# Differential attention: value products of a unit's first three groups follow their transposes by four groups, not three

## The chip, the cores and the metric

The kernel runs on one core of one Trainium2 chip. The metric is the device time of one execution in microseconds (us). Five engines work beside each other, each through its own queue in order: TensorE (PE in the profile, its weight loads PEld), VectorE (DVE), ScalarE (ACT), GpSimd (POOL) and SyncE (SP), which issues DMA transfers. They wait for one another through semaphores.

## The reference

The program is one step of a two-layer backbone over 2048 latent and 256 prompt tokens. Each layer has three head groups side by side; the change touches the first, differential attention with 4 heads:

```python
s = jnp.einsum('bqhcd,bkhcd->bhcqk', qblk, k).astype(jnp.float32) * scale
p = jax.nn.softmax(s, axis=-1)
w = p[:, :, 0] - lam * p[:, :, 1]
return jnp.einsum('bhqk,bkhd->bqhd', w.astype(v.dtype), v)
```

Every head has two score matrices (c = 0 and 1, of 64 channels each). Their softmaxes are combined into one weight matrix w, and w times the values (128 channels) is the output, which is then normalised and scaled. A latent query sees 2048 latent and 256 context keys, 2304 in all; a prompt query sees the 256 prompt keys.

## The kernel before

**Units.** Attention of a layer is cut into 36 units (list `units`): 4 heads, and of each head 8 blocks of 256 latent queries and, in the fifth place, one block of 256 prompt queries. Units are numbered from 0; units 4, 13, 22 and 31 are the prompt units.

**Scores.** `scores(i)` makes a latent unit's scores in 12 chunks: 2 query tiles j, 2 score matrices c, 3 pieces of 768 keys. A chunk is 4 matmuls into a psA buffer (line 882; psA has two buffers), which VectorE evicts with a running minimum (line 885). After three chunks comes the minimum over them, nb (line 889), and one exponential over 2304 columns on ScalarE, which also gives the sum z (line 890). After both matrices of a query tile, `combine` forms cf from the sums (reciprocal, line 935; product, line 936) and adds the second matrix to the first in three column sections: VectorE (line 945), ScalarE with GpSimd (lines 949 and 953), GpSimd alone (lines 952 and 953).

**Turns and products.** The combined weights lie with queries on the partitions, so they are transposed in groups of 256 keys. `turn(i, g)` makes the 4 transposes of a group (line 968) into one of three psT banks in rotation, and copies them out: for groups 0 to 5 a rounded part wh (ScalarE, line 977) and the rest wl (VectorE, line 978), each in a ring of three buffers; for groups 6 to 8 one f32 copy wf (ScalarE, line 973), two buffers. `product(i, g)` multiplies them with the values: 6 matmuls for a split group (lines 999 to 1001), 4 matmul passes for an f32 group (line 992). All nine products of a unit accumulate in one psT bank, `tb[0]`. The last one is followed by ScalarE's copy of this bank to oT (line 1007), so the next unit's first product has to wait for that copy. A unit's groups are taken in the order `ORDER`; the text calls their turns the 1st to the 9th. Groups 6, 7 and 8 are the 3rd, 6th and 9th.

**Output.** The last product also puts `output` on the list `later`, due two ticks on: two transposes of oT (line 1013) into the next of the three rotating banks, the copy ob, sums of squares, and GpSimd's scale; `finish`, due three ticks after it, multiplies and stores.

**What sets the order.** The loop behind `for _ in stepper` emits one chunk (one step of `scores`) at a time and adds `RATE` = 0.75 to a credit; with a credit of 1 it calls `advance`, which emits one turn and then, if more than `BACK` = 3 turns are waiting for their product, the product of the oldest. So 12 chunks go with 9 turns, and a product follows its own turn by three turns. After every `advance` the tick is raised by one, and what in `later` is due is emitted. The matmuls and transposes are pinned (`pin`): TensorE runs them in the order in which they are emitted. The instructions of VectorE and ScalarE in attention aren't pinned; the compiler's planner orders them. Scores run ahead of the turns of the same unit by one unit and some steps (`LAG`).

Of the kernel before, what the change touches and what calls it, by code (L numbers as in the profile page):

```python
# [13 lines left out]
F32R = mybir.dt.float32r  # L14
# [5 lines left out]
P = 128  # L20
# [19 lines left out]
DEFER = 3  # L40
ORDER = (0, 1, 6, 2, 3, 7, 4, 5, 8)
BACK = 3
SIDE = (1.02, 0.45)
SIDE_FROM = 2

# [32 lines left out]
def hybrid_backbone(ctx: ExitStack, tc: tile.TileContext, ins, outs):  # L78
# [8 lines left out]
    def nm(s):  # L87
        uid[0] += 1
        return f"{s}_{uid[0]}"
# [249 lines left out]
    for l in range(DEPTH):  # L339
# [266 lines left out]
        def sw_tiles(t):  # L606
            if t >= NT:
                return [NT + 2, NT + 3], 0
            b0, b1 = max(t - 1, 0), min(t + 1, NT - 1)
            return list(range(b0, b1 + 1)) + [NT, NT + 1], (b1 + 1 - b0) * P  # L610
# [104 lines left out]
        items = deque((t, i) for t in range(NALL) for i in range(len(sw_tiles(t)[0])))  # L715
        turned, later, ready = deque(), deque(), {}
# [87 lines left out]
        def v_slot(h, i):  # L804

            if i == 2:
                return (xslot, yslot)[h % 2][:, 6912:7680].rearrange("p (t d) -> p t d", d=P)
            o = (2 * h + i) % 3 * 1536
            return vslot[:, o:o + 1536].rearrange("p (a t d) -> p a t d", a=2, d=P)
# [5 lines left out]
        def p_slot():  # L815
            v = vslot[:, 4608:5632]
            return (v[:, 0:512].rearrange("p (c n) -> p c n", c=2),
                    v[:, 512:1024].rearrange("p (a t n) -> p a t n", a=2, t=2))
# [11 lines left out]
        def load_v(h, i):  # L830
            v1 = v_slot(h, i) if i == 2 else v_slot(h, i).bitcast(F32)
            if i == 2:
                hs = slice(h * P, (h + 1) * P)
                nc.sync.dma_start(out=v1[:, 0:4], in_=vfscr[l][:, :, hs].rearrange("t p d -> p t d"))
                nc.sync.dma_start(out=v1[:, 4:6],
                                  in_=c_dv[0, l].rearrange("(t p) h d -> p t h d", p=P)[:, :, h, :])
                return
            for a in range(2):
                nc.sync.dma_start(out=v1[:, a], in_=vscr[l][a, 6 * i:6 * i + 6, :, h * P:(h + 1) * P]
                                  .rearrange("t p d -> p t d"))  # L840
# [116 lines left out]
        def turn_bank():  # L957
            n_t[0] += 1
            return tb[1 + n_t[0] % 3]

        def turn(i, g):
            h, p = units[i]
            st = state[i]
            pt = turn_bank()
            for kk in range(2):
                for j in range(2):
                    o = (2 * kk + j) * P
                    pin(nc.tensor.transpose(out=pt[:, o:o + P],  # L968
                                            in_=st["s"][j][:, (2 * g + kk) * P:(2 * g + kk + 1) * P],
                                            identity=ident))  # L970
            if g >= 6:
                wh, wl = at.tile([P, 512], F32, tag="wf", name=nm("wf"), bufs=2), None
                nc.scalar.activation(wh, pt, AF.Copy)
            else:
                wh = at.tile([P, 512], F32R, tag="wh", name=nm("wh"), bufs=3)
                wl = at.tile([P, 512], F32R, tag="wl", name=nm("wl"), bufs=3)
                nc.scalar.activation(wh, pt, AF.Copy)  # L977
                nc.vector.tensor_tensor(wl, pt, wh.bitcast(F32), op=ALU.subtract)  # L978
            st[g] = wh, wl
            if g == groups(i)[-1]:  # L980
                free.extend(st["e"])

        def product(i, g):
            h, p = units[i]
            po = tb[0]
            wh, wl = state[i].pop(g)
            for kk in range(2):
                k = 2 * g + kk
                cs = slice(kk * 256, (kk + 1) * 256)
                last = g == groups(i)[-1] and kk == 1  # L990
                if g >= 6:
                    pin(nc.tensor.matmul(po[:, 0:256], v_slot(h, 2)[:, k % 6, :], wh[:, cs],  # L992
                                         start=False, stop=last))
                    continue
                if p < 8:
                    vh, vl = (v_slot(h, k // 6)[:, a, k % 6, :] for a in range(2))
                else:
                    vh, vl = (p_slot()[1][:, a, k, :] for a in range(2))
                pin(nc.tensor.matmul(po[:, 0:256], vh, wh[:, cs], start=(k == 0), stop=False))  # L999
                pin(nc.tensor.matmul(po[:, 0:256], vh, wl[:, cs], start=False, stop=False))  # L1000
                pin(nc.tensor.matmul(po[:, 0:256], vl, wh[:, cs], start=False, stop=last))
                if p == 7 and h < 3 and k == 5:
                    load_v(h + 1, 1)
            if last:
                st = state.pop(i)
                oT = at.tile([P, 256], F32, tag="oT", name=nm("oT"), bufs=2)
                nc.scalar.activation(oT, po[:, 0:256], AF.Copy)  # L1007
                later.append((tick + 2, lambda: output(h, p, st["ez"], oT)))

        def output(h, p, ez, oT):  # L1010
            pt = turn_bank()
            for j in range(2):
                pin(nc.tensor.transpose(out=pt[:, j * P:(j + 1) * P],
                                        in_=oT[:, j * P:(j + 1) * P], identity=ident))
            ss = at.tile([P, 16], F32, tag="ss", name=nm("ss"), bufs=3)[:, 0:2]
            ob = at.tile([P, 256], F32, tag="ob", name=nm("ob"), bufs=2)
            nc.scalar.activation(ob, pt[:, 0:256], AF.Copy)
            for j in range(2):
                js = slice(j * P, (j + 1) * P)
                nc.scalar.activation(oT[:, js], ob[:, js], AF.Square, accum_out=ss[:, j:j + 1])  # L1020
            nc.gpsimd.tensor_scalar(ss, ss, 1.0 / P, None, op0=ALU.mult)
            nc.gpsimd.tensor_tensor(ez, ez, ss, op=ALU.add)
            nc.gpsimd.tensor_tensor(ez, ez, mhalf.to_broadcast([P, 2]), op=ALU.pow)

            def finish():
                ov = ob.rearrange("p (j n) -> p j n", j=2)
                nc.gpsimd.tensor_tensor(ov, ov, ez.unsqueeze(2).to_broadcast([P, 2, P]), op=ALU.mult)
                rows = slice(2 * p * P, (2 * p + 2) * P)
                nc.sync.dma_start(out=oscr[l][rows, h * P:(h + 1) * P].rearrange("(j p) n -> p j n", p=P),
                                  in_=ov)  # L1030

            later.append((tick + DEFER, finish))

        def groups(i):
            return ORDER if units[i][1] < 8 else (0,)
# [45 lines left out]
        def p3_proj(i, a):  # L1081
# [4 lines left out]
            for k in range(KC):  # L1086
                if i >= SIDE_FROM:
                    due += SIDE[half] * (1 if k else 2)
                while due >= 1.0:
# [178 lines left out]
        at = Pool(tc, f"at{l}", side=near)  # L1268
# [6 lines left out]
        items = deque((i, g) for i in range(len(units)) for g in groups(i))  # L1275
        turned, later = deque(), deque()
# [3 lines left out]
        def advance():  # L1280

            if not items and not turned:
                return False
            if items:
                i, g = items[0]
                if at_ready.get(i, step + 1) > step:
                    return False
                turn(*items.popleft())
                turned.append((i, g))
            if len(turned) > BACK or not items:  # L1290
                product(*turned.popleft())
            return True

        for _ in stepper:
            credit = min(credit + RATE, 2.0)
            while credit >= 1.0 and advance():
                tick += 1
                credit -= 1.0
                while later and later[0][0] <= tick:
                    later.popleft()[1]()  # L1300
# [6 lines left out]
        while advance() or later:  # L1307
            if tick % 2 == 0:
                next(soon, None)
            tick += 1  # L1310
            while later and later[0][0] <= tick:
                later.popleft()[1]()
# [144 lines left out]
```

## Time and profile before

| what | value |
|---|---|
| median of 3 runs | 3640.16 us (3638.21 to 3643.04) |
| the profiled execution, its own time | 3639.05 us |
| span of the profiled execution, first to last instruction | 3637.2 us |
| mean granted TensorE clock | 0.991 |
| TensorE busy | 3507.7 us (96%) |
| VectorE busy | 2266.0 us (62%) |
| ScalarE busy | 1928.8 us (53%) |
| GpSimd busy | 1692.3 us (47%) |

The span is one execution recorded instruction by instruction; the 1.85 us between it and the execution's own time lie around it. Busy times are unions over the instructions of an engine. Matmuls are pipelined, with ends that are modelled: two rows of TensorE can overlap, so the start of a row and the idle time that it names in square brackets, with the engine and line that ended it, say more than its length. A wait is put down to the releaser that came last; very short pauses are not listed as waits.

### The profile page before, as it was taken

The numbers are of one execution on the slowest core, as the hardware profiler recorded it, in microseconds if no ns is written. First come the engines' busy times: TensorE is split into PE (matmuls) and PEld (weight loads), VectorE is DVE, ScalarE is ACT, GpSimd is POOL, SyncE is SP. The second block draws the span as 40 slices with busy tenths as digits, with TensorE's granted clock in tenths as the row PEclk, the third lists the DMA queues.
The fourth block names the chain that finished last, engine by engine and source line by source line (L and its number), as shares of the span: only waits on it lengthen the run. The fifth ranks groups of instructions, "written<-read, shape, count | busy, mean of one in ns | idle before, by whom it ended". The sixth has DMA issues, their size and how long they took to land.

```text
span 3637.2 us, 56156 instructions
## 1 busy us (share of the span) xinstructions
PE 3507.7 (96%) x20512; PEld 3043.4 (84%) x20512; DVE 2266.0 (62%) x4780; ACT 1928.8 (53%) x3192; POOL 1692.3 (47%) x1212
## 2 busy tenths in 40 slices
PE   8999999999999999999999999999999999999999
PEld 4788787888888898888878888889888889988887
DVE  3545665763588888885544232276437888888644
ACT  4432124653588888883223222266437888888511
POOL 3333233235477777762223232232436777777421
PEclk9999999999999999999999999999999999999999
DMA  7656557436412121226646454553533122111453
GB/s 255 195 167 197 173 171 216 128 108 210 124 44 81 46 84 57 69 62 228 223 154 179 139 167 125 163 153 117 179 128 106 61 63 83 48 57 55 143 182 116
DMA packets 397156, 477.83 MB, mean 131 GB/s; under 512 B 38353, under 2 KB 309969, under 8 KB 394321
## 3 DMA queue, kind: packets, MB, share of 16 engines
q1 hardware_dynamic: 385360, 462.71, 40.4%
q10 hardware_dynamic: 11520, 11.54, 0.9%
q8 instruction: 162, 2.65, 0.3%
q14 instruction: 114, 0.93, 0.1%
HBM read 314.75 MB, written 159.38 MB: 130 GB/s over the span
## 4 chain that ended last, share of the span: by engine, by line
PE 74%; DVE 10%; ACT 3%; POOL 3%; issue 3%; DMA 1%; SPq 1%; POOLq 0%; ACTq 0%; DVEq 0%
PE psA L882 10%; PE psT L293 7%; PE psT L295 7%; PE psT L294 7%; PE psT L968 5%; PE psA L293 3%; PE psA L295 3%; PE psA L294 3%; PE psT L301 3%; PE psT L303 3%; PE psT L302 3%; PE psT L992 3%; DVE W L885 2%; PE psT L692 2%; PE psT L999 2%
## 5 line engine op out<-in xcount | busy, mean ns | idle before, releaser
L349 POOL TENSOR_TENSOR hl<-h,hh 128x1024 fp32r<-128x1024 f32 x144 | 354.1, 2459 | 518.5 <-ACT hh L348 409.5
L885 DVE TENSOR_SCALAR_CACHE_REDUCE W<-psA 128x768 f32<-128x768 f32 x474 | 445.8, 951 | 87.6 <-PE psA L882 80.9
L882 PE MATMUL psA<-W,W 128*128 128x512 f32 (+1 forms) x1920 | 425.8, 352 | 17.8 <-DVE W L885 13.2
L890 ACT ACTIVATE W<-W,nb 128x2304 f32<-128x2304 f32 x158 | 351.0, 2221 | 78.2 <-DVE nb L889 77.3
L882 PEld LDWEIGHTS psA<-W,W 128*128 128x128 f32 x1920 | 301.1, 189 | 64.8 <-DVE W L885 24.2
L293 PE MATMUL psT<-W,hh 128*128 128x512 f32 (+1 forms) x864 | 312.3, 362 | 14.3 <-ACT hh L348 9.0
L885 DVE TENSOR_SCALAR_CACHE_REDUCE spool<-psA 128x768 f32<-128x768 f32 x294 | 276.7, 952 | 78.1 <-PE psA L882 55.7
L295 PE MATMUL psT<-W,hl 128*128 128x512 f32 (+1 forms) x864 | 308.8, 358 | 3.7 <-POOL hl L349 3.6
L294 PE MATMUL psT<-W,hh 128*128 128x512 f32 (+1 forms) x864 | 307.9, 356 | 0.1
L968 PE MATMUL psT<-ident,W 128*128 128x128 f32 x1616 | 291.2, 273 | 8.5 <-POOL W L953 6.7
L978 DVE TENSOR_TENSOR wl<-psT,wh 128x512 fp32r<-128x512 f32 x392 | 265.1, 683 | 20.8 <-ACT wh L977 20.0
L348 ACT ACTIVATE hh<-h 128x1024 fp32r<-128x1024 f32 x144 | 151.9, 1055 | 234.6 <-PE psT L294 137.3
L999 PE MATMUL psT<-wh,W 128*128 128x256 f32 x784 | 253.6, 323 | 13.1 <-ACT oT L1007 13.1
L882 PE MATMUL psA<-W 128*128 128x512 f32 (+1 forms) x1152 | 255.4, 351 | 9.5 <-DVE spool L885 5.4
L977 ACT ACTIVATE wh<-psT 128x512 fp32r<-128x512 f32 x392 | 225.5, 588 | 54.8 <-PE psT L968 53.8
L890 ACT ACTIVATE spool<-spool,nb 128x2304 f32<-128x2304 f32 x98 | 217.7, 2221 | 62.8 <-DVE nb L889 62.5
L952 POOL TENSOR_SCALAR W<-W,cf 128x768 f32<-128x768 f32 x70 | 162.6, 2322 | 188.5 <-DVE cf L936 73.9
L293 PE MATMUL psT<-W,mh 128*128 128x512 f32 x576 | 229.6, 399 | 4.8 <-ACT mh L1346 4.8
L293 PE MATMUL psA<-W,hh 128*128 128x512 f32 x576 | 229.7, 399 | 0.0
L968 PEld LDWEIGHTS psT<-ident,W 128*128 128x128 f32 x1616 | 202.7, 140 | 29.4 <-POOL W L953 7.8
L295 PE MATMUL psA<-W,hl 128*128 128x512 f32 x576 | 226.7, 394 | 0.0
L295 PE MATMUL psT<-W,ml 128*128 128x512 f32 x576 | 226.4, 393 | 0.0
(258 smaller groups left out, 9592.8 us busy)
## 6 DMA issues: line engine op xcount, KB each, us to landing
h<-hscr SPq DMA_DIRECT2D x126, 512.0 KB, 4.0
W<-qscr SPq DMA_DIRECT2D x288, 128.0 KB, 2.7
ws<-in_w_in SPq DMA_DIRECT2D x88, 256.0 KB, 3.7
kscr<-kst SPq DMA_DIRECT2D x160, 128.0 KB, 3.2
qscr<-qst SPq DMA_DIRECT2D x72, 256.0 KB, 2.8
szscr<-th SPq DMA_DIRECT2D x72, 256.0 KB, 2.1
qb<-qbscr SPq DMA_DIRECT2D x144, 128.0 KB, 2.9
W<-kscr SPq DMA_DIRECT2D x16, 1152.0 KB, 5.8
```

The source lines that it names most:

```text
L293: nc.tensor.matmul(out, ah[:, ks], w[:, 0, k, :n], start=(k == 0), stop=False)
L294: nc.tensor.matmul(out, ah[:, ks], w[:, 1, k, :n], start=False, stop=False)
L295: nc.tensor.matmul(out, al[:, ks], w[:, 0, k, :n], start=False, stop=(k == KC - 1))
L349: nc.gpsimd.tensor_tensor(hl, h32, hh.bitcast(F32), op=ALU.subtract)
L882: pin(nc.tensor.matmul(pa[:, o:o + wd], q[:, c, a, j * P:(j + 1) * P], ks[:, ch * 768 + o:ch * 768 + o + wd], start=(a == 0), stop=(a == 1)))
L885: nc.vector.tensor_scalar(sc_t[:, ch * 768:(ch + 1) * 768], pa[:, 0:768], -0.125, None, op0=ALU.mult, op1=ALU.min, accum_out=mn[:, ch:ch + 1])
L890: nc.scalar.activation(sc_t, sc_t, AF.Exp, bias=nb[:, j, c:c + 1], scale=-1.0, accum_out=z[:, j, c:c + 1])
L952: eng.tensor_scalar(s[1][:, sl], s[1][:, sl], cf, None, op0=ALU.mult)
L968: pin(nc.tensor.transpose(out=pt[:, o:o + P], in_=st["s"][j][:, (2 * g + kk) * P:(2 * g + kk + 1) * P], identity=ident))
L977: nc.scalar.activation(wh, pt, AF.Copy)
L978: nc.vector.tensor_tensor(wl, pt, wh.bitcast(F32), op=ALU.subtract)
L999: pin(nc.tensor.matmul(po[:, 0:256], vh, wh[:, cs], start=(k == 0), stop=False))
```

## The change

A new constant `AHEAD` = 3 and a helper `back` make the distance between a turn and its product depend on the group's place in the unit: for the first three groups of a unit a product is emitted only when more than four turns are waiting, for the others when more than three are. The rings of wh and wl get a fourth buffer. In one unit this gives: no product with the 4th turn, products of the 1st and 2nd group with the 5th and 6th turn, products of the 3rd and the 4th group together with the 7th turn, and from there on the old distance.

```diff
 BACK = 3
+AHEAD = 3
...
-                wh = at.tile([P, 512], F32R, tag="wh", name=nm("wh"), bufs=3)
-                wl = at.tile([P, 512], F32R, tag="wl", name=nm("wl"), bufs=3)
+                wh = at.tile([P, 512], F32R, tag="wh", name=nm("wh"), bufs=4)
+                wl = at.tile([P, 512], F32R, tag="wl", name=nm("wl"), bufs=4)
...
-            if len(turned) > BACK or not items:
+            if not items:
+                product(*turned.popleft())
+            while turned and len(turned) > back():
                 product(*turned.popleft())
             return True
+
+        def back():
+
+            i, g = turned[0]
+            return BACK + (groups(i).index(g) < AHEAD)
```

## Rows read from the trace of the kernel before

**Rows 1.** Stretches, layer 0 attention: us; busy PE, PEld, DVE, ACT, POOL (instructions); clock; DMA; GB/s

```profile
974.40:1616.10 641.70, 621.58 (x4211) 565.23 (x4208) 553.60 (x1293) 545.27 (x830) 476.70 (x392) 1.00 0.21 63
```

**Rows 2.** Waits of TensorE, whole run: waiter, releaser, us in total, times, longest

```profile
PE psA L882 <- DVE W L885: 17.2, 32, 1.0
PE psT L999 <- ACT oT L1007: 13.1, 20, 1.2
PE psA L882 <- DVE spool L885: 9.7, 16, 1.9
```

**Rows 3.** Stretch table, one unit each of patterns 1, 2, 3 and 4

```profile
994.20:1015.70 21.50, 20.23 (x136) 17.91 (x134) 17.24 (x41) 17.14 (x25) 13.62 (x12) 1.00 0.11 31
1122.30:1143.20 20.90, 20.05 (x136) 18.12 (x135) 17.82 (x41) 17.48 (x26) 14.96 (x13) 1.00 0.31 102
1288.70:1308.30 19.60, 19.60 (x137) 18.14 (x136) 17.13 (x41) 17.16 (x26) 15.00 (x12) 1.00 0.27 90
1450.80:1471.10 20.30, 19.77 (x136) 18.02 (x135) 17.32 (x43) 16.89 (x25) 14.93 (x13) 1.00 0.24 67
```

**Rows 4.** TensorE in order of time, pattern 2: start, us, what, idle before

```profile
1128.04 0.60 PE L968 MATMUL psT<-ident,spool 128*128 128x128 f32 x4
1129.15 0.39 PE L999 MATMUL psT<-wh,W 128*128 128x256 f32 x1 [0.52 <-ACT oT L1007]
...
1129.97 0.38 PE L1013 MATMUL psT<-ident,oT 128*128 128x128 f32 x2
1130.11 1.66 PE L882 MATMUL psA<-W 128*128 128x512 f32 x8
1131.60 0.60 PE L968 MATMUL psT<-ident,spool 128*128 128x128 f32 x4
1131.96 0.36 PE L999 MATMUL psT<-wh,W 128*128 128x256 f32 x1
```

**Rows 5.** ScalarE in order of time, the same unit

```profile
1126.03 2.22 ACT L890 ACTIVATE W<-W,nb 128x2304 f32<-128x2304 f32 x1 [0.63 <-DVE nb L889]
...
1128.73 0.37 ACT L1007 ACTIVATE oT<-psT 128x256 f32<-128x256 f32 x1
```

**Rows 6.** Who waited for the copy oT (us, times); the output's weight load (ns)

```profile
  PEld psT L999: 17.8, 20
...
L1013 PEld LDWEIGHTS psT<-ident,oT x144: 137/139/144, 1001.2 to 3411.8; 128*128 128x128 f32 x144
```

**Rows 7.** TensorE in order of time, the same unit, later

```profile
1132.76 0.88 PE L882 MATMUL psA<-W 128*128 128x512 f32 x4
1133.47 0.60 PE L968 MATMUL psT<-ident,spool 128*128 128x128 f32 x4
1133.91 1.03 PE L992 MATMUL psT<-wf,W 128*128 128x256 f32 x4
1134.59 1.05 PE L882 MATMUL psA<-W 128*128 128x512 f32 x4
1135.47 0.60 PE L968 MATMUL psT<-ident,spool 128*128 128x128 f32 x4
```

**Rows 8.** VectorE in order of time, the same unit

```profile
1131.16 0.95 DVE L885 TENSOR_SCALAR_CACHE_REDUCE W<-psA 128x768 f32<-128x768 f32 x1
...
1135.68 0.96 DVE L885 TENSOR_SCALAR_CACHE_REDUCE W<-psA 128x768 f32<-128x768 f32 x1 [1.04 <-PE psA L882]
...
1139.39 0.16 DVE L935 RECIPROCAL cf<-z 128x1 f32<-128x1 f32 x1
...
1141.40 0.94 DVE L885 TENSOR_SCALAR_CACHE_REDUCE spool<-psA 128x768 f32<-128x768 f32 x1
```

**Rows 9.** TensorE in order of time, a unit of pattern 4

```profile
1460.48 1.57 PE L882 MATMUL psA<-W 128*128 128x512 f32 x8
```

**Rows 10.** VectorE in order of time, the same unit of pattern 4

```profile
1459.73 0.95 DVE L885 TENSOR_SCALAR_CACHE_REDUCE W<-psA 128x768 f32<-128x768 f32 x1
...
1461.39 0.96 DVE L885 TENSOR_SCALAR_CACHE_REDUCE W<-psA 128x768 f32<-128x768 f32 x1 [0.71 <-PE psA L882]
```

## Prediction

> **What bounds the kernel now.** I read the stretch table first. The attention stretch of layer 0 lasts 641.70 us and layer 1 has its like, so attention is some 1283 us of the run, and the change acts only there. TensorE is busy for 621.58 us of it at a granted clock of 1.00, VectorE for 553.60 and ScalarE for 545.27 [rows 1]. TensorE is the bound, with 20 us idle per layer; VectorE has some 14% to spare, but not at every place.
>
> The table of waits says what the idle is [rows 2]. Score chunks waited 48 times for VectorE's eviction, 17.2 and 9.7 us, because psA has two buffers. Products waited 20 times for the copy oT, 13.1 us. Going through the matmuls in order of time I put each wait to the turn (1st to 9th of its unit) ahead of it. Of the chunk waits 31, with 17.9 us, stand after a 9th turn (3.0 us of it at the end of layer 0), 10 with 4.7 us after a 6th, and none after a 4th or 5th. Of the oT waits 18 stand after a 4th turn, ahead of a unit's first product, and two after a 3rd.
>
> The stream repeats, in five patterns that differ in the turns that two chunks follow. Of each layer's 32 latent units, 4 are of pattern 1 (units 0 to 3), 8 of pattern 2 (5 to 12), 8 of pattern 3 (14 to 21), 8 of pattern 4 (23 to 30) and 4 of pattern 5. One unit of each of the first four lasts 21.50, 20.90, 19.60 and 20.30 us, with 1.27, 0.85, 0.00 and 0.53 us of TensorE idle [rows 3]. Pattern 3 runs at TensorE's own pace; the others stall somewhere.
>
> **The wait the change aims at.** In a unit of pattern 2 the transposes of the 4th turn start at 1128.04; the unit's first product follows only at 1129.15, after 0.52 us of idle, then the output's two transposes at 1129.97, then two chunks [rows 4]. ScalarE shows why oT is late: an exponential started at 1126.03 and took 2.22 us, so the copy started at 1128.73 [rows 5].
>
> **Part 1: the first product leaves this place.** It goes behind the next turn. But `output` is due two ticks after the last product, counted in calls of `advance`, and the tick count doesn't change. So behind the 4th turn stands now the pair of transposes that read oT themselves, and TensorE's matmuls are pinned in this order. Nothing in the change makes ScalarE's copy earlier. The output's transposes then wait for the same copy until the same moment: the wait changes its owner, and I put **0 us** for it (bounds: 0, and -13.1 if it went wholly).
>
> At this place the Trainium skill's page "TensorE: Matmul & The Clock Gate" (section "Step-by-step: what each phase is for") says that weight loads are pulled ahead of matmuls in flight. By it a product's load of V would be done under the wait, while an output's load is oT itself, so that each of 20 moved waits would cost 139 ns more, an estimate of +2.8 us, or 3643 in place of 3641. The trace has it otherwise: in the same 20 waits the product's own weight load sat idle too, 17.8 us in all [rows 6], so by the row it is 0, and I take the row.
>
> **Part 2: the new order of blocks.** Starts give the cost of a block by what follows. Turn to product is 0.36 us, product to output 0.82, product to chunk 0.80, output to chunk 0.14 [rows 4, 7]; a turn ahead of an f32 product takes 0.44, the f32 product 0.68, and the chunk behind it 0.88 where one behind a split product takes 0.71 [rows 7]. Old order, 4th to 7th turn, without the chunks' own 0.71: 0.36+0.82+0.14+0.07 (what the pair after an output takes over 2 x 0.71), 0.36+0.80, 0.44+0.68+0.17, 0.36+0.80 = 5.00. New order: 0.44+0.14+0.07, 0.36+0.80, 0.36+0.80, 0.44+0.68+0.80 = 4.89, plus x for a split product right behind an f32 product, which no row shows. x lies between 0 and 0.17, what a chunk pays there. I take 0.08, as a product pays part of such a start behind a turn already: -0.03 a unit, **-2 us** for 64 units (bounds -7 and +4).
>
> **Part 3: chunks come earlier.** This is the part that costs. From the 4th to the 7th turn TensorE has one product less behind it, so the chunks between reach TensorE about 0.8 us sooner, while VectorE frees psA when it did. Pattern 2: after the wait the pair starts at 1129.29 instead of 1130.11, the chunk of 1132.76 at 1131.94. It needs the eviction that started at 1131.16 and took 0.95 [rows 8], and waits for 0.17 us; nothing is marked as idle ahead of this eviction, VectorE was at work, so an earlier chunk doesn't bring it forward. 16 units x 0.17 = 2.7. Pattern 4: the pair of 1460.48 [rows 9] starts at 1459.77, and its second chunk at 1460.48 needs the eviction of 1459.73, which ended at 1460.68 [rows 10]: 0.20 us, x 16 = 3.2. Pattern 1: the chunk after the 6th turn already waits; TensorE comes some 0.7 earlier and VectorE gains about half of it, as the eviction ahead is behind a ScalarE result: 0.35 lost for 6 units, 2.1 (bounds 0 and 0.75 each). Pattern 3: slack everywhere, 0. Pattern 5 and the units next to a prompt unit: 2 (bounds 0 and 7). Sum **+10 us**. If VectorE gained nothing anywhere, the same slack, read over all 64 units, gives +22, of which 11 remain once a later wait of the same unit has swallowed its share; if it gains all, 0.
>
> **Part 4: what comes back.** Earlier chunks are also earlier work for an engine that then waits. In pattern 2 VectorE idled 1.04 us ahead of the eviction at 1135.68 [rows 8], and this eviction leads to the next exponential. It would come about 0.6 us sooner. The reciprocal for that unit half stands at 1139.39, behind two evictions, with the combine after it and then the eviction at 1141.40, for which the chunk after the 9th turn waits: of the 0.85 us of idle of this unit 0.52 are the oT wait, and the other 0.33 are this one [rows 3, 4, 8]. If the reciprocal and the combine move ahead of an eviction, that wait goes. Pattern 4 is alike: 0.71 us idle ahead of 1461.39, and 0.53 us of wait after the 9th turn [rows 3, 10]. All such waits after a 9th turn, without the end of layer 0, are 14.9 us. VectorE's instructions aren't pinned, their order is the planner's; no row shows which it will choose, so I take half, **-7.5 us** (bounds -14.9 and 0).
>
> **At no cost.** The fourth buffer of wh and wl: no row shows a wait on these rings, and with three the fifth split turn would overwrite a weight whose product is still to come. Queues: `output` and its `finish` (POOL's normalisation, SP's store) keep their ticks. The one DMA issued inside a product, `load_v(h + 1, 1)`, hangs on group 2, fourth in ORDER, whose distance stays three; no SP or POOL instruction is passed. The drain at the end of a layer gives out one product per call as before. A prompt unit's single product is delayed by one turn too, but its output stays behind the next unit's first product; oT waits next to it stay.
>
> **Sum.** 0 - 2 + 10 - 7.5 = +0.5 us on the profiled execution's 3639.05, which is its span of 3637.2 and 1.85 around it. The median of the runs is 1.1 above it: 3640.16 + 0.5 is **3641**.
>
> **Rivals.**
> (a) The order on VectorE follows the earlier exponentials in patterns 1, 2 and 4, and the waits after the 9th turn go wholly; of the new waits some 3 us remain. -2 + 3 - 14.9 = -14, so 3626; where only one pattern follows, some 3632. For it: idle of 1.04 and 0.71 us ahead of the evictions in question. Against: the combine runs beside POOL's and each place shown must change order.
> (b) The oT wait truly goes, 13.1 us: 3627. Against it: the output stands ahead of the moved product by its tick. This is the case in which the change does what it says; that it does not is part of my forecast.
> (c) Slower: VectorE's order stays as it is. TensorE stalls ahead of the chunk after the 5th or 6th turn, and pays the moved product later, behind the 6th f32 product, where no idle time takes it. The net bound of part 3, +11: 3651. It decides from the point where the slack of that chunk is under the 0.8 us by which it comes earlier. Against: in pattern 3 (16 units) the slack is enough.
>
> **How the numbers follow.** 0.2% of this time is 7.3 us, about what a measurement can tell from no change; that makes the limits 3632.9 and 3647.4. Forecast, within them: 0.44. (a) 0.24 and (b) 0.07, both faster by more: 0.31. (c), slower by more: 0.25. The range runs from (b)'s 3627, which leaves out about half of (a), to (c)'s 3651; some 0.18 is left out.
>
> **What would show it.** No wait of the first product on oT in the new profile, and the output's transposes waiting for it about 18 times, some 10 to 13 us: part 1. Wait of chunks after the 5th and 6th turn up from 4.7 us by some 10: part 3. Waits after the 9th turn down from 17.9 us: part 4. Units of pattern 3 at 19.6 us still: part 2. I am wrong if the output's transposes don't wait, or if an oT copy comes earlier on ScalarE because its neighbours moved.

## The result and the profile after

| | before | after |
|---|---|---|
| median of 4 runs each, same chip | 3640.58 us (3638.21 to 3643.04) | 3675.53 us (3671.71 to 3688.76) |
| ratio of the runs, 95% interval | 1 | 1.0114 (1.0099 to 1.0129) |
| span of the profiled execution | 3637.2 us | 3674.0 us |
| mean granted TensorE clock | 0.991 | 0.985 |

The change is slower by about 1%, above the end of my range (3651 us). The ratio on record isn't the quotient of the medians, which is 1.0096; by both the kernel is slower, and its fastest run is above the slowest of before. From line 43 on the lines of the new kernel are one higher than before, from 1294 on eight; an experiment's edit shifts the lines behind it once more.

The attention stretch of layer 0 in the stretch table (us; busy PE, PEld, DVE, ACT, POOL; clock; DMA; GB/s) answers to [rows 1]:

```profile
975.20:1634.70 659.50, 628.43 (x4202) 570.78 (x4200) 549.78 (x1294) 541.11 (x829) 479.55 (x390) 0.99 0.20 61
```

It is 17.8 us longer, and layer 1's is 17.4 us longer by the same measure: 35.2 of the span's 36.8 us. TensorE's idle time grew from 20.1 to 31.1 us, and its busy time by 6.9 us for the same matmuls of attention. So there are two things to find, idle time and slower matmuls. The waits of TensorE, whole run (waiter, releaser, us in total, times, longest), answer to [rows 2]:

```profile
PE psT L1014 <- ACT oT L1008: 17.2, 30, 1.2
PE psT L1000 <- ACT oT L1008: 15.8, 8, 2.9
PE psA L883 <- DVE W L886: 14.9, 21, 2.0
...
PE psT L969 <- POOL spool L954: 9.1, 2, 4.8
...
PE psA L883 <- DVE spool L886: 6.7, 12, 1.7
```

The first line is the handed-over wait that I forecast. The second and fourth are new: a product that waits 2 us a time, eight times, and two turns that wait for GpSimd. The chunk waits, third and last line, fell from 26.9 to 21.6 us.

A table by unit says where these are. It takes the start of each unit's first transposes from the trace; a unit's length is the distance to the next. Given is the length with the change minus the length before, summed over both layers (us; a unit is named by its number within its layer). The last unit of a layer, 35, has no next one and isn't in the table: measured on to the last output transposes of each layer, attention is 41.1 us longer, and the stage between the two layers gives 5.2 us back. The other columns belong to experiments below.

| units | after | prompt back | prompt alone | copy on VectorE | steady |
|---|---|---|---|---|---|
| 5, 14, 23, 32 (behind a prompt unit) | +19.8 | +0.9 | +44.0 | +4.0 | -1.7 |
| 29, 30 | +11.6 | -1.0 | -0.1 | +10.7 | 0.0 |
| 16 to 20 (pattern 3) | +6.1 | +6.1 | 0.0 | +6.1 | 0.0 |
| 21 | +4.3 | +5.8 | 0.0 | +4.4 | 0.0 |
| 6 to 10 (pattern 2) | -3.8 | -3.7 | -0.5 | -3.9 | -3.9 |
| 24 to 28 (pattern 4) | -3.8 | -3.3 | +0.2 | -4.1 | -3.4 |
| all others | +1.0 | +1.0 | +1.6 | +3.2 | +0.1 |
| sum | +35.2 | +5.8 | +45.2 | +20.4 | -8.9 |

**Behind a prompt unit.** A prompt unit has a single group, which counts among its first three, so its product too is one turn later. Before, around unit 14, it stood behind the unit's 3rd turn at 1233.28, and ScalarE copied it to oT at 1235.48, behind an exponential and the copy wf; the unit's own first product at 1236.06 didn't wait (start, us, what; TensorE and then ScalarE):

```profile
1233.28 0.36 PE L999 MATMUL psT<-wh,W 128*128 128x256 f32 x1
...
1236.06 0.36 PE L999 MATMUL psT<-wh,W 128*128 128x256 f32 x1
```

```profile
1235.48 0.37 ACT L1007 ACTIVATE oT<-psT 128x256 f32<-128x256 f32 x1
```

Now, in order of time (with the idle before in brackets), TensorE and then ScalarE:

```profile
1235.60 0.36 PE L1000 MATMUL psT<-wh,W 128*128 128x256 f32 x1
...
1240.64 0.58 PE L1000 MATMUL psT<-wh,W 128*128 128x256 f32 x1 [2.92 <-ACT oT L1008]
...
1242.09 1.48 PE L883 MATMUL psA<-W 128*128 128x512 f32 x4
1243.37 0.41 PE L969 MATMUL psT<-ident,spool 128*128 128x128 f32 x1
...
1244.00 0.37 PE L1000 MATMUL psT<-wh,W 128*128 128x256 f32 x1
```

```profile
1236.97 1.16 ACT L950 ACTIVATE spool<-spool,cf 128x1024 f32<-128x1024 f32 x1
1238.01 2.22 ACT L891 ACTIVATE W<-W,nb 128x2304 f32<-128x2304 f32 x1
...
1240.20 0.38 ACT L1008 ACTIVATE oT<-psT 128x256 f32<-128x256 f32 x1
```

The prompt product comes at 1235.60, behind the 4th turn. Its copy has missed the gap ahead of the combine and the exponential and gets its turn at 1240.20, 4.6 us after the product's start. All products share the bank `tb[0]`, so the unit's first product, now behind the 5th turn, stands 2.92 us idle.

**The matmuls behind it are slow.** The stretch table shows the granted clock (the figure before the last two):

```profile
1238.00:1240.00 2.00, 0.00 (x0) 0.00 (x0) 1.26 (x3) 2.00 (x2) 2.00 (x3) 1.00 0.50 147
1240.00:1242.00 2.00, 1.36 (x6) 1.36 (x7) 0.69 (x1) 1.07 (x4) 2.00 (x2) 0.63 0.00 0
1242.00:1244.00 2.00, 2.00 (x10) 1.81 (x9) 0.40 (x1) 0.00 (x0) 1.92 (x3) 0.52 0.00 0
1244.00:1246.00 2.00, 2.00 (x16) 1.87 (x16) 0.65 (x3) 1.31 (x5) 1.41 (x4) 1.00 0.00 0
```

TensorE does nothing from 1238 to 1240, and then its clock is near 0.5, the 1.2 GHz level, until 1244. From the product to the chunk it takes 1.45 us (1240.64 to 1242.09) where [rows 4, 7] give 0.80, the chunk 1.28 against 0.71, the turn 0.63 against 0.36: 1.49 us lost. With the wait that is 4.4 us, and unit 14 is 4.28 us longer.

**Unit 29.** GpSimd in order of time, after:

```profile
1520.09 2.67 POOL L953 TENSOR_SCALAR W<-W,cf 128x768 f32<-128x768 f32 x1
1526.04 2.40 POOL L1342 TENSOR_TENSOR o<-o,sz 128x1024 f32<-128x1024 f32 x1 [3.28 <-DMA o<-oscr]
1528.41 4.10 POOL L954 TENSOR_TENSOR spool<-spool,W 128x1024 f32<-128x1024 f32 x2
```

and before:

```profile
1508.56 2.22 POOL L952 TENSOR_SCALAR W<-W,cf 128x768 f32<-128x768 f32 x1 [1.34 <-PE psA L882]
1510.86 4.21 POOL L953 TENSOR_TENSOR spool<-spool,W 128x768 f32<-128x768 f32 x2
1515.03 4.75 POOL L1334 TENSOR_TENSOR o<-o,sz 128x1024 f32<-128x1024 f32 x2
```

Line 1342 is no part of this attention's path: it is the first work of the stage that follows attention (`xo_load` multiplies a tile of the stored output). It isn't pinned, and the planner had put it on GpSimd's queue early, behind the combine's two adds. With the change it stands between the combine's scaling and its adds. There it waits 3.28 us for a DMA, and the adds behind it come 5.65 us late. TensorE needs them:

```profile
1532.56 0.48 PE L969 MATMUL psT<-ident,spool 128*128 128x128 f32 x1 [4.27 <-POOL spool L954]
```

Layer 1 has the same with 4.83 us. Around it the clock is low again, 0.57 in the mean of the 8 us from 1530 on:

```profile
1530.00:1538.00 8.00, 5.44 (x20) 4.85 (x21) 1.66 (x4) 2.67 (x5) 7.92 (x5) 0.57 0.38 118
```

### The profile page after: what moved, and what is told of

Its sections match the earlier page's. It is cut to its first block, busy times and chain, and to the rows that moved or that the text cites. A ratio compares the mean times of both kernels' runs of the same rounds, so it can differ in the third digit from the quotient of the medians.

```text
span 3674.0 us, 56143 instructions
## 1 busy us (share of the span) xinstructions
PE 3526.0 (96%) x20512; PEld 3058.8 (83%) x20512; DVE 2261.8 (62%) x4780; ACT 1921.9 (52%) x3192; POOL 1699.1 (46%) x1212
## 4 chain that ended last, share of the span: by engine, by line
PE 73%; DVE 8%; ACT 7%; issue 3%; POOL 2%; DMA 1%; SPq 0%; ACTq 0%; POOLq 0%; DVEq 0%
PE psA L883 10%; PE psT L294 7%; PE psT L296 7%; PE psT L295 7%; PE psT L969 4%; PE psA L296 3%; PE psA L295 3%; PE psA L294 3%; PE psT L302 3%; PE psT L304 3%; PE psT L303 3%; PE psT L993 3%; ACT W L891 2%; PE psT L693 2%; DVE W L886 2%
## 5 line engine op out<-in xcount | busy, mean ns | idle before, releaser
L1000 PE MATMUL psT<-wh,W 128*128 128x256 f32 x784 | 261.4, 333 | 15.8 <-ACT oT L1008 15.8
```

## The experiments

My theory: the loss sits in these places, about 20 us behind the prompt units and 11 to 13 us at the GpSimd multiply, with a remainder in patterns 1 and 3 that patterns 2 and 4 nearly give back. The rival: products a turn later cost everywhere, and these are only the places where it shows.

### Prompt units back at three groups

```diff
-            return BACK + (groups(i).index(g) < AHEAD)
+            return BACK + (units[i][1] < 8 and groups(i).index(g) < AHEAD)
```

> The changed kernel, but the single product of a prompt unit follows its transposes by three groups again. Two theories share the 35 us lost. Theory A: the loss sits in a few places. The unit after each prompt unit (the 6th, 15th, 24th and 33rd of a layer) waits 0.86 to 2.92 us for the prompt unit's copied output (oT), 7.9 us a layer, and with the half-clock stretches behind two of these waits those units and their followers are about 11 us a layer longer, 22 us in both. The GpSimd multiply of the output stage that stands in the middle of a combine in the 30th unit (another 5.3 and 5.8 us) also goes back behind its adds in this kernel, because the planner places it anew. So A expects 3675 - 22 - 11 = 3642 us, give or take 6, no oT wait before a unit's first product, and no stretch at half clock inside attention. Theory B, the rival: turning the products later costs everywhere (blocks and combines run a turn earlier for all units), and the waits seen are only where it shows; then this edit moves 8 prompt products of some 420 us' worth of products and the time stays above 3665 us.

Measured: 3647.05 us beside 3634.72 of before, ratio 1.0031 (1.0019 to 1.0042); span 3645.3. The only wait of a product for oT left is one of 1.2 us a layer that before has too; units 14 and 29 are within 0.8 us of before or shorter (column "prompt back"). The time lies within the theory's 3642 us, give or take 6, and the rival's 3665 us is out. But beside the before of the same runs 12.3 us remain, where the theory left some 2: 5.8 us in the table, pattern 3 and unit 21 against patterns 2 and 4, and 6.4 us in the last unit of the two layers, for which I had no term. This kernel cures both places at once, since the planner's order on GpSimd went back too; the next runs take them apart.

### The GpSimd multiply alone, and its control

```diff
-            nc.gpsimd.tensor_tensor(o, o, sz, op=ALU.mult)
+            m = nc.gpsimd.tensor_tensor(o, o, sz, op=ALU.mult)
+            if t < 2:
+                pin(m)
```

In the changed kernel:

> The changed kernel, with the first two GpSimd multiplies of the output stage of each layer held in program order, that is behind all of attention's GpSimd work instead of inside the combine of the 30th unit. Theory A: the 30th unit loses its 4.27 and 4.83 us waits for the combined chunk and gets 5.3 + 5.8 = 11 us shorter; the two multiplies, 2.40 us each, now stand in front of the first output tile's transposes, which costs 0 to 5 us a layer. So 3664 us, at most 3674; the difference to the kernel before with the same hold is 35 - 11 = 24 us. Theory B (general slowing): the wait for that chunk is replaced by a later one, the difference to the kernel before with the same hold stays 35 us.

In the kernel before:

> The kernel before, with the same hold on the first two GpSimd multiplies of the output stage: the control that prices the hold itself. There the multiplies stood behind the adds of the 30th unit and nothing on TensorE waited for them, so nothing is won; 4.8 us of multiplies a layer come in front of the first output tile. 3640 to 3650 us by both theories.

Measured: 3678.24 us, ratio 1.0119 (1.0105 to 1.0132), and 3649.79 us, ratio 1.0038 (1.0025 to 1.0050). The first is above what I expected, the second at the upper end of it and 15 us above its before, since the hold costs more than the 0 to 5 us a layer I had given it. The waits of TensorE show its price, the same in both kernels; the control's line is:

```profile
PE psA L1344 <- POOL o L1334: 12.4, 2, 6.2
```

The early multiply on GpSimd was worth having: put behind attention it holds up the first output tile by 6.2 us a layer. Against its own control the changed kernel's span is 3675.1 - 3650.2 = 24.9 us longer (expected 24), not 36.8: by these executions the place of the multiply is worth 11.9 us. By the medians it is less, 28.5 us in place of 35.0, so its size is uncertain by 5 us or more. Attention itself is 22.1 us longer than before, not 35.2, and units 29 and 30 are 3.0 us shorter than before, not 11.6 longer.

### Both edits

> The changed kernel with both edits: prompt units at three groups, and the two GpSimd multiplies held. What is left of the change is the four-group distance in the other 32 units of each layer and the rings. Theory A: 35 - 22 - 11 = about 2 us is left over the kernel before with the same hold (3642 to 3652 us). Theory B: at least 25 us is left.

Measured: 3654.70 us, ratio 1.0054 (1.0042 to 1.0067). Its span is 2.7 us above the control's, by the medians it is 4.9 us; attention is 4.6 us longer than before by the measure of the table. The two places together are nearly all of the loss.

### The rings alone

```diff
-                wh = at.tile([P, 512], F32R, tag="wh", name=nm("wh"), bufs=3)
-                wl = at.tile([P, 512], F32R, tag="wl", name=nm("wl"), bufs=3)
+                wh = at.tile([P, 512], F32R, tag="wh", name=nm("wh"), bufs=4)
+                wl = at.tile([P, 512], F32R, tag="wl", name=nm("wl"), bufs=4)
```

> The kernel before with the rings wh and wl of four buffers, all distances at three: the second part of the change alone. No row of before shows a wait on these rings, and every engine's instructions stand in the same order as in the kernel before; only addresses differ. Theory A (the loss is in the late product of prompt units and in the GpSimd multiply): the same time as before within 0.2%, 3640 us. Theory C (the wider rings themselves cost, by where they put the buffers): up to 11 us slower, what was left over when prompt units went back to three groups.

Measured: 3636.85 us beside 3634.50, ratio 1.0004 (0.9995 to 1.0013). These runs show no cost of the rings.

### The late product of prompt units alone

```diff
-            return BACK + (groups(i).index(g) < AHEAD)
+            return BACK + (units[i][1] == 8)
```

> The complement of the kernel with prompt units put back: here only the prompt unit's product follows by four groups, all others by three. The output stage's GpSimd multiplies stand behind the adds as in before. Theory A: the four units behind a prompt unit in each layer wait for oT (some 8 us a layer) and run a stretch at half clock, so the 15th and 24th unit of a layer are about 4 us longer each and the time is 15 to 22 us over the kernel before, some 3658 us. Theory B (the loss comes from the ordinary units' distance and the prompt unit only shows it): within 0.2% of before.

Measured: 3679.33 us, ratio 1.0120 (1.0106 to 1.0134); span 3677.7. The place is right and my size was half of it: in attention this part alone costs more than the whole change, 45.2 against 35.2 us, and by the runs' ratios as much. The column "prompt alone" has all of the loss in units 5, 14, 23 and 32. TensorE in unit 14:

```profile
1244.77 0.39 PE L1000 MATMUL psT<-wh,W 128*128 128x256 f32 x1 [4.09 <-ACT oT L1008]
```

Here the ordinary unit's first product keeps its place behind the 4th turn, where the late prompt product now stands too, so it waits for the whole way from product to copy. In the changed kernel it had moved a turn itself, which hid some of it. I had taken the waits of the changed kernel as the price of the part; they were what another part had left of it.

### The prompt unit's copy on VectorE

```diff
-                nc.scalar.activation(oT, po[:, 0:256], AF.Copy)
+                if p == 8:
+                    nc.vector.tensor_copy(oT, po[:, 0:256])
+                else:
+                    nc.scalar.activation(oT, po[:, 0:256], AF.Copy)
```

> The changed kernel, but the copy oT of a prompt unit is made by VectorE and not by ScalarE; the products stand where the change puts them, and the GpSimd multiply stays in the middle of the combine. If the wait is ScalarE's queue (the copy of 0.38 us stood behind a combine of 1.16 us and an exponential of 2.22 us that had started 2.2 us before), the waits of the first product behind prompt units, 15.8 us, fall to under 4 us, and the half-clock stretches behind them go: 15 to 22 us less than the changed kernel, some 3656 us. If the wait is due to the product's being late as such, or VectorE's queue is as long (an eviction takes 0.95 us there, and two may stand ahead), at least half of the 15.8 us stays and the time is above 3665 us.

Measured: 3657.90 us, ratio 1.0066 (1.0053 to 1.0078). The wait of the products behind prompt units:

```profile
PE psT L1000 <- DVE oT L1009: 4.0, 4, 1.1
```

4.0 us in place of 15.8, with all products where the change puts them. So it is ScalarE's queue that made the late product dear. (The columns of the table are of the profiled execution, here the slowest of five, 3666.07 us; in it attention is 14.8 us shorter than in the changed kernel.) The longest of these waits is 1.1 us, and around it the clock stays up:

```profile
1240.00:1242.00 2.00, 0.92 (x8) 0.68 (x7) 2.00 (x4) 2.00 (x3) 2.00 (x1) 1.00 0.77 230
1242.00:1244.00 2.00, 2.00 (x17) 1.91 (x17) 1.08 (x3) 1.86 (x4) 2.00 (x3) 1.00 0.02 6
```

Units 29 and 30 are still 10.7 us longer, as the multiply still stands between combine and adds.

### Only where units got shorter

```diff
-            return BACK + (groups(i).index(g) < AHEAD)
+            return BACK + (groups(i).index(g) < AHEAD and (4 < i < 11 or 22 < i < 29))
```

> The four-group distance only in the units where the changed kernel's trace shows units getting shorter one after the other: the 6th to 11th and the 24th to 29th of each layer (0.3 to 0.4 us each). All other units, prompt units too, at three groups. If these gains are the units' own, it is 24 x 0.35 = 8 us faster than before, 3632 us, that is 0.2% faster; if each gain is only what a longer unit before it has given up, it is within 0.1% of before or slower by the edges, where the distance changes.

Measured: 3626.46 us beside 3634.50, ratio 0.9977 (0.9968 to 0.9986), faster than both kernels. The attention stretch of layer 0 is 637.00 us at a clock of 1.00, 4.7 less than [rows 1]. The gain lies in the units themselves (column "steady": -0.2 to -0.6 us each), and the edges cost nothing.

### The output one tick later

If the wait for oT is a price wherever it stands, an output that also stands a turn later should be rid of it.

```diff
-                later.append((tick + 2, lambda: output(h, p, st["ez"], oT)))
+                later.append((tick + 3, lambda: output(h, p, st["ez"], oT)))
```

With prompt units back at three groups:

> The changed kernel with prompt units at three groups, and the output of every unit due three ticks after its last product instead of two, so that it stands one more turn behind the copy oT. The wait for oT that the change handed from the first product to the output's transposes (15.5 us in 30 waits in the kernel with prompt units put back alone) is now behind neither. If that wait was a real price, it goes, and up to 15 us with it: 3632 us, against 3647 for the prompt units alone; above all the units of the pattern without idle time (the 17th to 21st of a layer), 0.6 us longer each with the change, are at 19.6 us again. If the wait only stood in front of another one (a score chunk that would have waited for VectorE anyway), chunk waits grow by as much and the time stays within 0.2% of 3647 us.

With the four-group distance in units 5 to 10 and 23 to 28 only:

> The four-group distance only in the 6th to 11th and the 24th to 29th unit of each layer (3626 us, 0.2% faster than before, with the output at two ticks), and the output three ticks after the last product. In those 24 units neither product nor output then waits for oT; in the other 40 the first product still does (7.0 us), as nothing makes the copy earlier. If the output's wait in the 24 units is a price of its own (0.4 us each), 10 us faster again: 3616 us. If chunks wait instead: the same as at two ticks.

In the kernel before:

> The kernel before, with the output three ticks after the last product: the control for the later output. The first product still waits for oT (13.1 us) and VectorE's evictions are as they were. The chunk pair no longer stands behind the output there and comes 0.14 us earlier, the output's ScalarE and GpSimd work one turn later. Within 0.2% of before, 3636 us, if the output's place alone is worth nothing; any gain seen in the two kernels with later output has to be larger than what this one shows.

Measured: 3659.31 us, ratio 1.0065 (1.0053 to 1.0078); 3633.55 us, ratio 0.9996 (0.9987 to 1.0005); and 3643.45 us, ratio 1.0022 (1.0013 to 1.0031). All three are worse than with the output at two ticks, and none of my figures was right, the control's included. In the first the oT wait is nearly gone (1.3 us left), and another has come. The waits of TensorE:

```profile
PE psT L969 <- DVE nb L890: 19.7, 18, 1.7
```

In a unit of pattern 3, TensorE, VectorE and ScalarE:

```profile
1261.72 0.66 PE L969 MATMUL psT<-ident,W 128*128 128x128 f32 x4 [0.96 <-DVE nb L890]
```

```profile
1260.09 0.96 DVE L886 TENSOR_SCALAR_CACHE_REDUCE spool<-psA 128x768 f32<-128x768 f32 x1 [0.50 <-PE psA L883]
...
1260.97 0.69 DVE L979 TENSOR_TENSOR wl<-psT,wh 128x512 fp32r<-128x512 f32 x1
```

```profile
1257.34 2.21 ACT L891 ACTIVATE W<-W,nb 128x2304 f32<-128x2304 f32 x1
...
1259.55 0.58 ACT L978 ACTIVATE wh<-psT 128x512 fp32r<-128x512 f32 x1
```

The turn waits for one of the three rotating psT banks. Two later users, the output and another turn, hold the other two; the bank it needs is read last by VectorE's subtraction wl, which follows ScalarE's wh, which stands behind the same kind of exponential that had held oT. (The releaser that the view names, nb, is the short minimum right behind the subtraction.) But the exponential isn't the last thing in the way: wh was out at 1260.13, and an eviction that stands ahead of wl in VectorE's order kept it until 1260.97. Without that eviction wl would have been done by 1260.82, an estimate from these rows, and most of the 0.96 us would not be there. In all 18 of these waits such an eviction stands ahead of wl. So the wait came back at another bank, and there by the order on VectorE.

By units the picture splits. In units 6 to 10, of pattern 2, the two kernels that have both the distance of four and the later output are 12.1 us shorter than before over both layers, 1.2 us a unit, where the output at two ticks gave 3.8 us; TensorE has no listed wait left in these units. There the later output was worth what I had hoped and more. In the kernel of the 24 units, units 12, 16 to 20 and 21, which have the later output with the distance of three, lose 3.7, 3.3 and 3.9 us, and units 24 to 28 gain 0.2 us in place of 3.4. A kernel with the later output in units 5 to 10 alone wasn't run.

## Why the prediction was wrong, step by step

**"At no cost" is the step that failed.** It had two sentences that cost the result.

"A prompt unit's single product is delayed by one turn too, but its output stays behind the next unit's first product; oT waits next to it stay." I looked at the output and not at the first product of the next unit, which waits for the same copy. The first half of it I had counted right: the product moves past a turn. But I didn't ask what ScalarE does between the old place and the new one; the answer was in the trace of before, an exponential of 2.2 us of the kind of [rows 5]. Measured: 19.8 us in the change, 44.0 us alone.

"... no SP or POOL instruction is passed." In the order in which the program emits instructions that holds. But unpinned ones stand where the planner puts them, and one that belongs to the next stage went into the middle of a combine. Measured: 11.9 us by the profiled executions. I had written for VectorE that its order is the planner's, and left GpSimd out. No row of before could show that it would move; that it stood unpinned inside attention, [rows 1]'s stretch, could be seen.

**No term for the clock.** All prices were worked out at a granted clock of 1.00, as all of [rows 1, 3] had it. A wait of 2.9 us cost 1.5 us more behind it.

**Part 1 (the wait changes its owner, 0 us)** was right in its mechanism: the output's transposes wait 17.2 us in 30, forecast 10 to 13 in some 18. In pattern 2 it is the same wait at the same place of the unit, 0.52 before [rows 4] and now:

```profile
1130.17 0.44 PE L1014 MATMUL psT<-ident,oT 128*128 128x128 f32 x2 [0.53 <-ACT oT L1008]
1130.37 1.64 PE L883 MATMUL psA<-W 128*128 128x512 f32 x8
1131.84 0.60 PE L969 MATMUL psT<-ident,spool 128*128 128x128 f32 x4
1132.20 0.36 PE L1000 MATMUL psT<-wh,W 128*128 128x256 f32 x1
...
1133.17 0.97 PE L883 MATMUL psA<-W 128*128 128x512 f32 x4
```

Its bounds of 0 and -13.1 lacked the other side. Pattern 3 had no such wait, and got one:

```profile
1301.27 0.44 PE L1014 MATMUL psT<-ident,oT 128*128 128x128 f32 x2 [0.46 <-ACT oT L1008]
```

```profile
1298.15 0.60 ACT L974 ACTIVATE wf<-psT 128x512 f32<-128x512 f32 x1 [1.25 <-PE psT L969]
1298.65 2.21 ACT L891 ACTIVATE W<-W,nb 128x2304 f32<-128x2304 f32 x1
...
1300.85 0.37 ACT L1008 ACTIVATE oT<-psT 128x256 f32<-128x256 f32 x1
```

Before, the copy stood behind the exponential and wf:

```profile
1295.11 0.38 ACT L1007 ACTIVATE oT<-psT 128x256 f32<-128x256 f32 x1
```

Now wf is ahead of the exponential, and the copy comes 0.62 us later in the unit (7.05 us behind the unit's first transposes in place of 6.43). The units that I had at 19.6 us still take 20.2, 6.1 us for 16 to 20 in both layers. The cause on ScalarE is read from the trace; no run undid it alone.

The price of the changed owner: where output and chunk start 0.14 us apart without a wait [rows 4], they start 0.20 apart behind one, so 0.06 us each, some 2 us for 30. I had taken 0 by [rows 6]. The Trainium skill's page "TensorE: Matmul & The Clock Gate" (section "Step-by-step: what each phase is for") has weight loads pulled ahead of matmuls in flight, from which I had estimated 0.139 us each; the trace lies between the two.

**Part 2 (order of blocks, -2 us)** can't be told apart from the rest: where nothing waits, pattern 4 now has a unit of 19.80 us with 19.80 busy, against 19.77 busy in [rows 3].

**Part 3 (earlier chunks, +10 us)** was mis-sized. In pattern 2 the one I had worked out came as forecast: the chunk needs the eviction that starts at 1132.16 and takes 0.94 us (below), and starts 0.97 us behind the product of 1132.20 where 0.80 is usual, 0.17 us. But chunk waits listed behind a 5th or 6th turn are 1.0 us in all, not the 4.7 of before plus 10; new ones stand behind the 1st turn, 5.5 us (4.0 of it in unit 21), and the 8th, 2.5 us. What I missed is that the same chunks' earlier end let VectorE's order change.

**Part 4 (what comes back, -7.5 us)** was right in size: waits behind a 9th turn went from 17.9 to 9.4 us. VectorE in pattern 2, which answers to [rows 8] (this unit runs 1.00 us later than there):

```profile
1132.16 0.94 DVE L886 TENSOR_SCALAR_CACHE_REDUCE W<-psA 128x768 f32<-128x768 f32 x1
...
1136.04 0.96 DVE L886 TENSOR_SCALAR_CACHE_REDUCE W<-psA 128x768 f32<-128x768 f32 x1 [0.51 <-PE psA L883]
...
1140.61 0.16 DVE L936 RECIPROCAL cf<-z 128x1 f32<-128x1 f32 x1
...
1141.45 0.94 DVE L886 TENSOR_SCALAR_CACHE_REDUCE spool<-psA 128x768 f32<-128x768 f32 x1
...
1142.33 0.82 DVE L946 SCALAR_TENSOR_TENSOR W<-W,cf,W 128x512 f32<-128x512 f32 x1
```

The idle of 1.04 us is 0.51, and the eviction behind it comes 0.64 us earlier in the unit; I had said 0.6. But the way was the other one: the reciprocal didn't come earlier (0.22 later), and the combine didn't move ahead of the eviction. The planner put the eviction ahead of the combine, so it comes 0.95 us earlier, and the chunk behind the 9th turn finds its buffer. So parts 3 and 4 together gave a gain where the patterns are steady, 0.4 us a unit, as rival (a) had it; the run with these units alone shows it as 0.23% of the kernel's time.

**Rivals.** (c), the slower one, had the wrong cause: not chunk stalls, which fell. My list held no rival with a copy that misses its gap on ScalarE, though the change delays the one product whose copy the next unit needs.

**What stays open.** Unit 21 is 2.2 us longer, with a chunk wait of 2.0 us behind its 1st turn, with and without the late prompt product; which order on VectorE or GpSimd makes it wasn't tried. Nor was it tried what makes the last unit of each layer 2.9 us longer. Nor was the clock's share measured by a run that changes the clock alone.

## What to carry to other kernels

When a step is moved behind another one, ask of every consumer of its result, and for every kind of unit, what the engine that hands the result on does between the old place and the new: a copy of 0.4 us that misses its gap waits for the 2.2 us instruction behind it. Special cases (here 4 prompt units of 36) deserve the check first, since they took about half of the loss, and a change that is good in the steady units and bad at the seams can be restricted to the former. Where a scheduler places unpinned work, look for instructions of a neighbouring stage in the stretch, above all such as wait for a DMA: here an edit elsewhere put one in front of work that was needed.

## What the runs showed that was not expected

- TensorE's clock went to 0.5 behind idle times of 2.92 and 4.27 us inside attention and stayed at 1.00 around one of 1.1 us, in the runs shown above. The length of a wait alone doesn't tell: in the trace of the changed kernel a wait of 1.94 us in unit 0 was followed by 0.50 (in the 2 us from 995 on), one of 2.00 us in unit 21 by 1.00 (in the 2 us from 1378 on).
- Removing the GpSimd multiply from attention cost 6.2 us of TensorE waiting a layer, more than the two multiplies' own 4.75 us: an instruction that looks misplaced was prefetched work.
- The later output took the wait off oT (15.5 us in 30 waits) and brought another at a turn's bank (19.7 us in 18) in patterns 1, 3 and 4, while pattern 2 got rid of all its waits: whether a moved wait comes back was decided by pattern.
